# Six input projections as seven block products each, in a stage ahead of attention, and attention fed from DRAM

## The chip, the cores and the metric

The kernel runs on one core of one Trainium2 chip. The metric is the device time of one execution in microseconds (us), the median of the runs. One execution was also taken with the hardware profiler; all rows in this text come from it. The engines are named as in the profile: PE is TensorE (PEld its weight loads), DVE is VectorE, ACT is ScalarE, POOL is GpSimd, SP is SyncE, whose queue (SPq) issues most DMAs.

## The reference, cut to what matters

One decoder block on 1024 tokens of width 1024, in float32. A normed input is projected to 6664 columns, split into queries, keys and values of two kinds of attention, memory queries and gates:

```python
h = rmsnorm(x, g_mix_norm[l])
proj = jnp.einsum('bsd,de->bse', h, w_in[l])
sb_q, sb_k, sb_v, fx_q, fx_k, fx_v, f_logit, m_q, gate_logit = split_columns(proj, SPLITS)
o_sb = stick_breaking_attention(...)      # 8 heads of 64; weights from products of 1 - sigmoid, strictly causal
fq, fk = rmsnorm(fx_q, g_fox_q), rmsnorm(fx_k, g_fox_k)     # per head
o_fox = forgetting_attention(fq, fk, fx_v, log_f)            # 8 heads of 64; causal softmax with a decay
o_mem = memory_attention(rmsnorm(m_q), rmsnorm(m_k), m_v)    # 4 heads of 128; 256 memory tokens
merged = gates[0] * (o_sb @ w_branch_sb) + gates[1] * (o_fox @ w_branch_fox) + gates[2] * (o_mem @ w_branch_mem)
x = x + merged @ w_out
x = x + relu(rmsnorm(x) @ w_ff_up) ** 2 @ w_ff_down
```

Each of sb_q, sb_k, sb_v, fx_q, fx_k, fx_v and m_q has 512 columns, the gates 3072, the forget logits 8.

## The kernel before, in words

**Precision.** Every operand is split into a rounded high part (an ACT copy) and a low part (a DVE subtraction, the remainder). A product takes three passes on PE: high by high, high by low, low by high. So each product tile costs three matmuls, and each operand tile one ACT and one DVE operation. Line 951 is the remainder of a weight tile (L950 its copy).

**Order.** `Machine` (lines 182 to 278) is a planner that runs while the kernel is built. Generators yield `Op(engine, cost, fn)`, `Get(place, n)` for buffers and events; the planner keeps a clock, gives each engine the ready operation with the earliest time (plus a lateness that the caller chose), and emits instructions in that order. Operations with `side=True` (projections, gates, branches) go to PE only when no attention work is ready there. The order is fixed when the kernel is built; on the chip each engine works through its list in order and waits where a result isn't there.

**Stages, by the profile's clock.** Up to about 120 us: norms of the tokens, transposes, the first values with the first keys of stick-breaking attention, the memory keys and values. 120 to 232: memory queries and memory attention (`mem_attention`). 232 to about 590: stick-breaking attention, four pairs of heads (`sb_tile`, `unit`). 620 to about 941: forgetting attention, four pairs (`fox_tile`, `unit`). Beside the attention run the projections for later pairs (`sb_projection`, `dense_values`, `dense_fox`) and the 24 gate blocks (`dense_gate`), then the first two branch products (`dense_branch`, to about 979). Then the last branch, the output projection, and the MLP, whose up and down products, like the output projection, are already done in seven block products (P1 to P7, Winograd's form of Strassen's scheme). These later stages are outside the change.

**Projections before.** Two forms. `dense_T` (gates, stick-breaking keys and queries) has weights stationary and 512 tokens moving, and leaves the result with features on the partitions. `natural_ops` (values, memory queries, forgetting queries and keys) has 128 tokens stationary and 256 columns moving. All of these matmuls are emitted by `products`, line 1040. Results go from the PSUM bank straight into attention's tiles in SBUF: the normed ones by a copy and a square on ACT (L628, L629), a reduction (L630), a reciprocal root (seed on DVE, three steps on POOL), a scaling (L692, L1324), four transposes on PE (L700, L1277), and a copy and remainder (L702, L703, L1289 to L1303).

**Attention.** A unit is one head and 256 queries (group g of 0 to 3); large units are g = 2, 3. For each 128 queries, `sb_tile` forms scores (L772, L773), masks the diagonal (L782), takes two sigmoids (L776, L777), scans a product from the right (L791) and multiplies (L795); `fox_tile` forms scores (L815, L816), masks (L823), takes maxima (L824 and small operations to L829), exponentials (L833), a reciprocal (L838) and a scaling (L846). `unit` then transposes the weights (L874), splits them (L879 on ACT, L881 on DVE), multiplies them with the values (L894) and stores the output (L912, L913, L915). One large and one small unit are in flight; `PACE` and `units` hold each unit back until a set amount of side work was done.

**Memory.** SBUF places are pools of tiles (`HT` head tiles, `EL`/`ES` attention rows, `VV` values, `WP` three pairs of split weights, `RAW` raw weights, `OO` outputs). PSUM has eight banks: three `PP`, two `SC`, two `TR`, one `PV`.

Of the kernel before, what the change touches and what calls it, by code (L numbers as in the profile page):

```python
# [43 lines left out]
def tile_hybrid_block(  # L44
# [40 lines left out]
    C = Pool("c", st=24, st16=8, ss=4)  # L85
# [35 lines left out]
    fk_scr = dram.tile([8, 4, S], F32, name="fk_scr", tag="fk_scr")  # L121
    x2_scr = dram.tile([S, D], F32, name="x2_scr", tag="x2_scr")
# [184 lines left out]
    mem_T = [tuple(A.t(tag, [P, D], F32R).rearrange("p (k s) -> p k s", k=KD) for tag in ("e", "r")) for _ in range(2)]  # L307

    def halves(w, cols):
        res = []  # L310
        for h in range(2):
            rows = slice(h * 512, (h + 1) * 512)
            pieces, off = [], 0
            for c0, n in cols:
                pieces.append((off, w[rows, c0:c0 + n]))
                off += n
            res.append(load_w(pieces, 4, off))
        return res
# [23 lines left out]
    ES, OO = tiles(A, "es", 2, 512), tiles(A, "o", 3, 512)  # L342
    EL, RR, HT = Places([]), Places([]), Places([])
    PH, PL, OB = tiles(A, "pth", 2, 512, F32R), tiles(A, "ptl", 2, 512, F32R), tiles(A, "ob", 2, 256)
    VV = tiles(A, "v", 2, 4096, F32R)
# [163 lines left out]
    def prologue():  # L509
# [12 lines left out]
        holder["B"] = B = Pool("b", h=20)  # L522
        HT.put(*(B.t("h", [P, 512], F32R) for _ in range(20)))


    mk_made, mv_made = ([Event() for _ in range(2)] for _ in range(2))
    mq_made, mem_over = {(h, half): Event() for h in range(4) for half in range(2)}, Event()
    mq_of, mkv = {}, {}
    kv_over = Event()

    def memory():
        v = VV.free.pop()
        mkv["kh"], mkv["kl"] = (v[:, i * 1024:(i + 1) * 1024].rearrange("p (h m) -> p h m", h=4) for i in (0, 1))
        mkv["vh"], mkv["vl"] = (v[:, i * 1024:(i + 1) * 1024].rearrange("p (j e) -> p j e", j=2) for i in (2, 3))
        for ev in [spawn(mem_attention(h, half), -20.0) for c in range(2) for half in range(2) for h in (2 * c, 2 * c + 1)]:
            yield ev
# [3 lines left out]
    def mem_attention(h, half):  # L540
# [46 lines left out]
        def block(j):  # L587
# [14 lines left out]
            if j == 0:  # L602
                pv[0] = yield Get(PV)
# [1800 lines left out]
```

## Time and profile before

| | |
|---|---|
| median of 3 runs | 1741.8 us (1741.77 to 1741.9) |
| the profiled execution | 1741.96 us |
| its span, first to last instruction | 1740.2 us |
| ACT busy | 884.1 us (51%) |
| POOL busy | 117.2 us (7%) |
| granted TensorE clock | 1.0 |
| HBM read, written | 142.64 MB, 57.15 MB |
| mean DMA rate | 116 GB/s |

How to read the rows: a group row gives line, engine, operation, output and inputs by the program's names, the shape and the count; behind the first bar the busy time of the group and the mean nanoseconds of one; behind the second bar the idle time of that engine just before such instructions and what ended it. A timeline row gives the start, the duration and the instruction. A wait row says which instruction waited for which, with the sum, the number of times and the longest in us. Matmuls are pipelined, so their durations overlap; the distance between starts is what one costs.

### The profile page before, as it was taken

How to read it: one execution, taken by the hardware profiler on the slowest of the kernel's cores; microseconds unless marked ns; L12 is line 12 of the kernel's file. 1: busy time of each engine (PE TensorE's matmuls, PEld its weight loads, DVE VectorE, ACT ScalarE, POOL GpSimd, SP SyncE). 2: the span in 40 equal slices, each digit the busy share in tenths (PEclk: the TensorE clock that was granted, in tenths of full speed). 3: DMA queues.
4: the chain of work that ended last, by engine and by line, in shares of the span. 5: the costliest groups of instructions: out<-in, count | busy, mean ns of one | idle time of the engine just before them, and what ended most of it. 6: DMA issues, size and time to landing. Idle time of an engine off the chain costs nothing.

```text
span 1740.2 us, 24835 instructions
## 1 busy us (share of the span) xinstructions
PE 1726.8 (99%) x9426; PEld 1476.1 (85%) x9426; DVE 1261.5 (72%) x2014; ACT 884.1 (51%) x1553; POOL 117.2 (7%) x301
## 2 busy tenths in 40 slices
PE   9999999999999999999999999999999999999999
PEld 9889989888988899899888887878888887888887
DVE  7524578677777567666887699887777776687875
ACT  6525575555566478767974236533333344333331
POOL 0101100000000000010000000111112120000000
PEclk9999999999999999999999999999999999999999
DMA  5241121122132311212354643144444476455531
GB/s 206 73 125 52 50 87 38 42 68 57 35 89 59 90 54 32 75 49 68 113 176 134 231 157 116 49 151 155 142 151 145 152 254 230 160 201 178 193 121 73
DMA packets 135561, 201.41 MB, mean 116 GB/s; under 512 B 9681, under 2 KB 73169, under 8 KB 135441
## 3 DMA queue, kind: packets, MB, share of 16 engines
q1 hardware_dynamic: 125584, 167.05, 29.9%
q0 software_dynamic: 9856, 32.78, 5.4%
q8 instruction: 74, 1.21, 0.3%
q14 instruction: 47, 0.38, 0.1%
HBM read 142.64 MB, written 57.15 MB: 115 GB/s over the span
## 4 chain that ended last, share of the span: by engine, by line
PE 82%; issue 7%; DVE 5%; ACT 2%; POOL 2%; DMA 1%; SPq 0%; POOLq 0%; DVEq 0%; ACTq 0%
PE pp L1040 36%; PE pp L2343 7%; PE pp L1673 6%; PE pv L894 4%; PE tr L2343 4%; PE sc L2343 4%; PE tr L874 3%; PE sc L1673 3%; PE pv L2343 2%; POOL s_scr L1690 1%; PE tr L1673 1%; PE tr L1916 1%; PE sc L772 1%; PE sc L815 1%; PE sc L773 1%
## 5 line engine op out<-in xcount | busy, mean ns | idle before, releaser
L1040 PE MATMUL pp<-hi,whi 128*128 128x512 f32 x496 | 199.1, 401 | 0.0
L1040 PE MATMUL pp<-hi,wlo 128*128 128x512 f32 x496 | 195.7, 395 | 0.0
L1040 PE MATMUL pp<-lo,whi 128*128 128x512 f32 x496 | 195.1, 393 | 0.0
L1040 PE MATMUL pp<-whi,hi 128*128 128x256 f32 (+1 forms) x640 | 183.3, 286 | 0.0
L1040 PE MATMUL pp<-whi,lo 128*128 128x256 f32 (+1 forms) x640 | 179.8, 281 | 0.2 <-DVE lo L487 0.2
L1040 PE MATMUL pp<-wlo,hi 128*128 128x256 f32 (+1 forms) x640 | 179.3, 280 | 0.0
L881 DVE TENSOR_TENSOR ptl<-tr,pth 128x512 fp32r<-128x512 f32 (+1 forms) x160 | 99.3, 631 | 43.2 <-ACT pth L879 42.5
L2343 PE MATMUL pp<-h,sop 128*128 128x512 f32 x540 | 128.7, 395 | 0.4 <-DVE sop L1609 0.4
L2343 PEld LDWEIGHTS pp<-h,sop 128*128 128x128 f32 x540 | 101.2, 188 | 25.5 <-DVE sop L1609 0.9
L879 ACT ACTIVATE pth<-tr 128x512 fp32r<-128x512 f32 (+1 forms) x160 | 86.3, 555 | 70.6 <-PE tr L874 39.1
L1673 PE MATMUL pp<-h,oh 128*128 128x512 f32 x384 | 120.9, 396 | 0.7 <-ACT cu L1759 0.6
L1040 PEld LDWEIGHTS pp<-wlo,hi 128*128 128x128 f32 x640 | 120.6, 188 | 0.9
L1040 PEld LDWEIGHTS pp<-whi,hi 128*128 128x128 f32 x640 | 120.6, 188 | 0.8
L1040 PEld LDWEIGHTS pp<-whi,lo 128*128 128x128 f32 x640 | 120.5, 188 | 0.4 <-DVE lo L487 0.4
L1040 PEld LDWEIGHTS pp<-hi,wlo 128*128 128x128 f32 x496 | 93.2, 188 | 22.6
L951 DVE TENSOR_TENSOR wlo<-raw,whi 128x1024 fp32r<-128x1024 f32 (+1 forms) x72 | 87.7, 1221 | 33.9 <-ACT whi L950 33.5
L1040 PEld LDWEIGHTS pp<-lo,whi 128*128 128x128 f32 x496 | 93.3, 188 | 16.8
L1040 PEld LDWEIGHTS pp<-hi,whi 128*128 128x128 f32 x496 | 93.4, 188 | 16.3
L791 DVE TENSOR_TENSOR_SCAN r<-r,sm 128x896 f32<-128x896 f32 (+3 forms) x64 | 86.2, 1351 | 12.9 <-ACT r L776 12.4
L950 ACT ACTIVATE whi<-raw 128x1024 fp32r<-128x1024 f32 (+1 forms) x72 | 76.2, 1061 | 34.1 <-DMA raw<-w_b 24.6
L1673 PEld LDWEIGHTS pp<-h,oh 128*128 128x128 f32 x384 | 71.8, 188 | 19.1 <-ACT cu L1759 1.5
L2261 ACT ACTIVATE h<-t 128x2048 fp32r<-128x2048 f32 x16 | 30.7, 1919 | 109.9 <-DVE t L1609 97.1
(425 smaller groups left out, 4281.1 us busy)
## 6 DMA issues: line engine op xcount, KB each, us to landing
ur<-s_scr SPq DMA_DIRECT2D x26, 1024.0 KB
raw<-w_in SPq DMA_DIRECT2D x42, 512.0 KB
raw<-w_up SPq DMA_DIRECT2D x60, 256.0 KB
s_scr<-s POOLq DMA_DIRECT2D x60, 256.0 KB, 2.7
g<-w_down SPq DMA_DIRECT2D x14, 1024.0 KB
gate_scr<-o SPq DMA_DIRECT2D x48, 256.0 KB
s_scr<-cu POOLq DMA_DIRECT2D x48, 256.0 KB, 2.9
o<-gate_scr SPq DMA_DIRECT2D x32, 256.0 KB
```

Source lines behind the costliest of these rows:

```text
L772: nc.tensor.matmul(sc[:, :m], q, pair.t["k1", b, ci][:, :m], start=True, stop=False)
L791: nc.vector.tensor_tensor_scan(out=rev, data0=rev, data1=zero.to_broadcast([P, n]), initial=1.0, op0=ALU.mult, op1=ALU.add)
L874: nc.tensor.transpose(tr[:, jj * 256 + a * P:jj * 256 + (a + 1) * P], es[a][:, j * P:(j + 1) * P], ident)
L879: yield Op("ACT", act_time(512 - lo_c), lambda: nc.scalar.activation(ph[:, lo_c:], tr[:, lo_c:], AF.Copy))
L881: yield Op("DVE", dve_time(512 - lo_c), lambda: nc.vector.tensor_tensor(pl[:, lo_c:], tr[:, lo_c:], f32(ph[:, lo_c:]), ALU.subtract))
L894: nc.tensor.matmul(pv[0][:, c_:256], v_of[key][:, j, h4, :], p_[:, jj * 256 + c_:(jj + 1) * 256], start=(k == 0 and n_ == 0 and i == 0), s ...
L950: yield Op("ACT", 0.03 + act_time(m), lambda: nc.scalar.activation(hi, raw, AF.Copy))
L951: yield Op("DVE", dve_time(m), lambda: nc.vector.tensor_tensor(lo, raw, f32(hi), ALU.subtract))
L1040: nc.tensor.matmul(ps, a_, b_, start=(first and i == 0), stop=(last and i == n - 1))
L1673: nc.tensor.matmul(ps, w[a_][:, k * P:(k + 1) * P], h[b_][k], start=(first and k == 0 and i == 0), stop=(last and k == 3 and i == 2), skip ...
L2261: nc.scalar.activation(top[k][0], raw, AF.Copy)
L2343: nc.tensor.matmul(ps, a_[:, c, qs], b_[:, c, :], start=(kind in ("P1", "P2", "P7") and c == 0 and i == 0), stop=(kind in ("P2", "P4", "P3 ...
```

## The change

The six projections sbk, sbq, mq, fxk, fxq and sbv become a stage of their own ahead of attention. Each is cut into halves of tokens, contraction and columns and done in seven block products P1 to P7 instead of eight. sbk and sbq keep the weights stationary (512 columns moving); the other four keep the tokens stationary (256 columns moving).

- `sums_T` forms the sums of token blocks (operands of P5, P6, P7 and, later, P4) once for all six.
- `unit_loads` and `unit_prep` load a unit's four weight blocks, form the four block sums on DVE and split the seven operands.
- `unit_products` emits the products; `unit_evict` copies banks to SBUF (`snap`) and adds the later ones; `unit_final` splits or norms and turns the results, which are stored to DRAM. `SN` is a pool of ten tiles for all of these.
- `load_pairs`, `load_v` and `memory` bring queries, keys and values back from DRAM by DMA alone, head by head.
- `forget` works on one half at a time in three `SN` tiles. Gate 8 takes the place of the first keys beside the first values, which are now fx0; fx1 follows.
- Attention begins when the stage ends (`second_part` opens its pools). `PACE` is gone; large and small units have four row tiles each, so two of each are in flight. `fox_tile` takes the maximum of each key stretch (up to 512 keys) by itself and corrects by the exponential of the difference. Memory attention runs after the keys of the first forgetting pair are loaded.
- PSUM in attention: two `PP` and two `PV` banks. `HT` has 23 tiles, four of them made of one `WP` pair.

```diff
-    A = Pool("a", v=2, pth=2, ptl=2, e=2, es=2, r=2, o=3, ob=2)
+    E = Pool("e", side="right", sn=10)
+    MT = Pool("mt", side="right", mt=4)
+    R = Pool("r", raw=4, s1=1)
...
+    def sums_T():
+        for k in range(4):
+            (b11, b12), (b21, b22) = (...)
...
+            yield Op("DVE", dve_time(512, 512, 512), first)
+            yield Op("DVE", dve_time(512, 512), second)
+            two = [spawn(both("P6", k, t2)), spawn(both("P5", k, t1), 2.0)]
+            yield Op("DVE", dve_time(512, 512), third)
+            two.append(spawn(both("P7", k, w_), 1.0))
...
     def fox_tile(pair, b, i, e):
-        scs = yield Get(SC, len(ch))
...
+        def chunk(ci, c, cols, u):
+            sc = yield Get(SC)
...
+            yield Op("PE", mm_time(cols, cols), scores)
+            yield Op("DVE", (0.22 if c + u == n else 0.0) + dve_time(u) + SMALL, maxima)
+            yield Op("ACT", act_time(u) + 0.17, lambda: nc.scalar.activation(
+                e[:, c:c + u], sc[:, :u], AF.Exp, bias=nx[:, ci:ci + 1], accum_out=l[:, ci:ci + 1]), table=AF.Exp)
+            SC.put(sc)
...
+        if two:
+            def most():
+                nc.vector.tensor_tensor(m[:, 0:1], nx[:, 0:1], nx[:, 1:2], ALU.min)
+            yield Op("DVE", SMALL, most)
+            yield Op("ACT", 0.22, lambda: nc.scalar.activation(f, mx, AF.Exp, bias=m[:, 0:1]), table=AF.Exp)
...
+                nc.vector.tensor_tensor(t_, l, f, ALU.mult)
+                nc.vector.tensor_tensor(m[:, 1:2], t_[:, 0:1], t_[:, 1:2], ALU.add)
+                nc.vector.reciprocal(t_[:, 0:1], m[:, 1:2])
+                nc.vector.tensor_scalar(f, f, t_[:, 0:1], None, ALU.mult)
...
     def units(large):
-        yield kv_over
-        for ev in mq_made.values():
-            yield ev
-        base = machine.side
+        yield ready
...
-                while machine.side - base < PACE[c] + (PACE[c + 1] - PACE[c]) * n / 8:
-                    yield Sleep(0.5)
-                spawn(unit(pair, b, g, es))
+                spawn(unit(pair, b, g, es), 0.0 if large else -6.0)
+
+    def load_pairs():
+        yield ready
+        for c, pair in enumerate(pairs):
...
+            for b in range(2):
+                got = yield Get(HT, 8 if fox else 6)
...
+                machine.fire(pair.made[b])
...
+    PROJ = ("sbk", "sbq", "mq", "fxk", "fxq", "sbv")
...
+    def unit_prep():
+        yield kv_taken
+        for u in PROJ:
+            for kind in KINDS:
...
+                    for out_, a_, b_, op in ((s1, a21, a22, ALU.add), (a21, a11, a21, ALU.subtract),
+                                             (a11, s1, a11, ALU.subtract), (a12, a12, a11, ALU.subtract)):
+                        yield Op("DVE", dve_time(1024), lambda: nc.vector.tensor_tensor(out_, a_, b_, op))
+                pair = yield Get(WP)
...
+                yield from split(pair[0][:, :1024], pair[1][:, :1024], src)
...
+    def unit_products(u, turned_w):
...
+            for kind in KINDS:
+                yield prepped[u, kind]
+                pair, w = p_ops[u, kind]
+                for q in range(2):
...
+                    if kind in ("P6", "P5", "P3"):
+                        yield snapped[u, {"P6": "P1", "P5": "P6", "P3": "P5"}[kind], q]
+                    if kind == "P4":
+                        yield added[u, "P5", q]
...
+    def hand_back():
+        for place in (PP, PP, SC, SC, PV, PV):
+            place.put((yield Get(BK)))
...
+    def second_part():
...
+        yield last_sums
+        yield prepped[PROJ[-1], "P4"]
+        holder["T"].close()
+        R.close()
+        opened("A", (HT, "h", 12, 512, F32R), (VV, "v", 2, 2048, F32R), (EL, "e", 4, D, F32), (RR, "r", 3, D, F32))
+        machine.fire(ready)
+        yield last_turn
+        for ev in proj_over:
+            yield ev
+        yield forgot
+        holder["T4"].close()
+        E.close()
+        opened("A2", (PH, "pth", 2, 512, F32R), (PL, "ptl", 2, 512, F32R), (OB, "ob", 2, 256, F32),
+               (ES, "es", 4, 512, F32), (OO, "o", 3, 512, F32), (HT, "h", 7, 512, F32R))
...
+    gates = [dense_gate(n, may_gate) for n in (*range(16, 24), *range(0, 8), *range(9, 16))]
+    h_tasks = [dense_values("fx0", C_FXV, None, first_gate), dense_values("fx1", C_FXV + 256, fn)]
...
+    h_tasks += kv_tasks
+    h_tasks += [unit_products(u, u in ("sbk", "sbq")) for u in PROJ]
     h_tasks += gates
...
-    PACE = [62 * min(c, 4) + 58 * max(c - 4, 0) + 14 * (c == 8) for c in range(9)]
```

More of the change, by code (lines that the diff above doesn't have):

```diff
@@ L971, in loader @@
     def loader(tasks):
-        two = False
         while tasks:
-            t = next((t for t in tasks if not (two and len(t.loads) == 2) and t.may()), None)
-            two = False
+            t = next((t for t in tasks if t.may()), None)
             if t is None:
@@ L1193, in sb_projection @@
[L1193 to L1204 removed]
+                evict(last, put(ps, t // 2), ps, SC)
```

861 lines of the change are left out of this document (476 added, 385 removed).

## The prediction

> **What bounds the kernel now.** I read the page first, then who made TensorE (PE) wait, then the pace of PE's instructions, then stretches of the span.
>
> ```profile
> span 1740.2 us, 24835 instructions
> ...
> PE 1726.8 (99%) x9426; PEld 1476.1 (85%) x9426; DVE 1261.5 (72%) x2014; ACT 884.1 (51%) x1553; POOL 117.2 (7%) x301
> ...
> PE 82%; issue 7%; DVE 5%; ACT 2%; POOL 2%; DMA 1%; SPq 0%; POOLq 0%; DVEq 0%; ACTq 0%
> ...
> L1040 PE MATMUL pp<-hi,whi 128*128 128x512 f32 x496 | 199.1, 401 | 0.0
> ...
> L1040 PE MATMUL pp<-whi,hi 128*128 128x256 f32 (+1 forms) x640 | 183.3, 286 | 0.0
> ```
>
> PE is busy for 99% of the span and carries 82% of the chain of waits. The two L1040 rows are one third each of the input projections (three passes per product): 3 x 496 matmuls of 512 columns and 3 x 640 of 256.
>
> A busy PE need not be a full one, so I looked at its waits (twelve rows, the first and the last shown) and at the starts of consecutive matmuls.
>
> ```profile
> PE tr L874 <- DVE ptl L881: 1.5, 1, 1.5
> ...
> PE sc L815 <- ACT e L833: 0.2, 1, 0.2
> ```
>
> ```profile
> 100.19 0.40 PE L1040 MATMUL pp<-hi,whi 128*128 128x512 f32 x1
> ...
> 103.70 0.39 PE L1040 MATMUL pp<-hi,whi 128*128 128x512 f32 x1
> ```
>
> ```profile
> 622.05 0.28 PE L1040 MATMUL pp<-whi,hi 128*128 128x256 f32 x1
> ...
> 626.55 0.28 PE L1040 MATMUL pp<-whi,lo 128*128 128x256 f32 x1
> ```
>
> ```profile
> 247.37 0.62 PE L874 MATMUL tr<-ident,e 128*128 128x128 f32 x4
> 247.75 0.36 PE L894 MATMUL pv<-pth,v 128*128 128x256 f32 x1
> ```
>
> Fifteen matmuls of 512 columns start within 3.51 us, so one costs 0.234 us, not the 0.40 it is shown to last. Between 622.05 and 626.55 there are 38 steps of 256 columns: 0.118 us each. Four transposes take 0.38 us, 0.095 each. The longest PE wait is 1.5 us. So what is taken from PE comes off the time, unless the work that remains stops arriving in time.
>
> ```profile
> 87.00:120.00 33.00, 32.55 (x190) 28.25 (x189) 10.09 (x10) 8.93 (x12) 0.45 (x3) 1.00 0.45 128
> 232.00:590.00 358.00, 357.93 (x2123) 313.67 (x2122) 273.60 (x404) 211.84 (x422) 4.11 (x13) 1.00 0.22 62
> ...
> 620.00:853.00 233.00, 232.72 (x1628) 215.28 (x1627) 163.98 (x409) 177.76 (x366) 16.44 (x72) 1.00 0.20 59
> 853.00:941.00 88.00, 85.31 (x476) 72.81 (x475) 74.11 (x176) 67.33 (x139) 0.00 (x0) 1.00 0.45 142
> ```
>
> The columns after the length are busy PE, PE's weight loads, VectorE (DVE), ScalarE (ACT), GpSimd, then granted clock, DMA share, GB/s. In the stick-breaking attention (232 to 590) DVE is 76% busy, in the forgetting attention (620 to 853) 70%, in its end (853 to 941) 84%. PE is full because projections and gates fill the gaps of attention there. That is the reserve which the change rearranges.
>
> **What the change does to PE.** A projection of 512 columns takes 192 matmuls of 512 columns (8 contraction tiles x 4 x 2 x 3 passes) or 384 of 256. With 7 block products it takes 7 x 2 x 4 x 3 = 168, or 336. Two units (sbk, sbq) run in the wide form: 2 x 24 x 0.234 = 11.2 us less. Four (mq, fxk, fxq, sbv) run in the narrow form: 4 x 48 x 0.118 = 22.7 us less. Together **33.9 us** less. The normed units turn 3 x 32 blocks, as many as the old code does for the same columns, and the columns of scores and values stay. So nothing is added on PE.
>
> **What the change adds beside PE**, priced with these rows.
>
> ```profile
> L881 DVE TENSOR_TENSOR ptl<-tr,pth 128x512 fp32r<-128x512 f32 (+1 forms) x160 | 99.3, 631 | 43.2 <-ACT pth L879 42.5
> L951 DVE TENSOR_TENSOR wlo<-raw,whi 128x1024 fp32r<-128x1024 f32 (+1 forms) x72 | 87.7, 1221 | 33.9 <-ACT whi L950 33.5
> L791 DVE TENSOR_TENSOR_SCAN r<-r,sm 128x896 f32<-128x896 f32 (+3 forms) x64 | 86.2, 1351 | 12.9 <-ACT r L776 12.4
> ...
> L824 DVE TENSOR_REDUCE st<-sc 128x1 f32<-128x512 f32 (+2 forms) x96 | 53.3, 556 | 14.5 <-PE sc L816 12.2
> ...
> L795 DVE TENSOR_TENSOR e<-e,r 128x895 f32<-128x895 f32 (+3 forms) x32 | 32.5, 1015 | 0.7
> ...
> L913 DVE TENSOR_TENSOR ob<-ob,pv 64x256 f32<-64x256 f32 x64 | 25.9, 404 | 15.3 <-ACT ob L912 14.7
> ...
> L823 DVE TENSOR_TENSOR sc<-sc,above 128x128 f32<-128x128 f32 x64 | 18.6, 290 | 9.6 <-PE sc L816 9.5
> L782 DVE TENSOR_TENSOR sc<-sc,above 128x128 f32<-128x128 f32 x64 | 18.4, 290 | 10.3 <-PE sc L773 10.2
> ...
> L795 DVE TENSOR_TENSOR es<-es,r 128x127 f32<-128x127 f32 (+3 forms) x32 | 15.4, 484 | 1.2
> ...
> L560 DVE TENSOR_REDUCE st<-sc 128x2 f32<-128x512 f32 x16 | 11.0, 685 | 6.4 <-PE sc L149 6.4
> ...
> L630 DVE TENSOR_REDUCE ss<-o 128x8 f32<-128x512 f32 x16 | 10.9, 680 | 10.8 <-ACT o L629 10.5
> L838 DVE RECIPROCAL st<-st 128x1 f32<-128x1 f32 x64 | 10.3, 161 | 4.8 <-ACT es L833 3.2
> ...
> L1324 DVE TENSOR_TENSOR r<-r,st 128x1024 f32<-128x1024 f32 x8 | 9.8, 1224 | 8.0 <-POOL st L368 8.0
> ...
> L703 DVE SCALAR_TENSOR_TENSOR h<-tr,sm,h 128x512 fp32r<-128x512 f32 x8 | 6.0, 750 | 5.8 <-ACT h L702 5.8
> ```
>
> ```profile
> 1014.56 0.68 DVE L1609 TENSOR_TENSOR g<-g 128x512 f32<-128x512 f32 x1
> ...
> 1016.96 0.68 DVE L1609 TENSOR_TENSOR cu<-g,cu 128x512 fp32r<-128x512 f32 x1
> ```
>
> In a dense stretch four such steps take 2.40 us: 0.60 us of DVE for an operation shown as 0.68. Sums of durations are thus up to 12% too high when the engine is full. I give both.
>
> *The token sums.* The sums of the halves and their splits are 40 operations of 512 columns before the units (40 x 0.68 = 27 us of DVE) and 16 later. They fall among the values and the memory keys; from 87 to 120 DVE is busy 10.1 of 33 us. Cost nothing; without that cover the third product (P6) would start late by what remains, at most 27 us.
>
> *Start of the units.* The first weight block needs an ACT copy and an L951 remainder (1.22 us) with a 5.6 us memory-value product left to cover it. Between 0 and some 3 us; I take **1.5**.
>
> *The three normed units (mq, fxk, fxq).* Per unit: 4 block sums and 7 remainders of 1024 columns, 11 x 1.22 = 13.4 us; six additions of a bank, 6 x 0.68 = 4.1; eight finals of a reduction (0.68), half an L1324 (0.61), an L703 (0.75) and two small operations (2 x 0.16), 8 x 2.36 = 18.9. That is 36.4 us of DVE beside 336 x 0.118 = 39.6 us of PE: 92%, or 81% at the dense pace. The forget gate falls into fxk with ten operations at 0.68 and two scans (1.35 as L791's mean): 9.5 us more, while it holds three of the ten SN tiles. Over three units 118.7 us of DVE stand against 118.8 of PE. Low end 0 (dense pace, 105 us), high end: DVE 85% busy at full durations, 118.7 / 0.85 = 140, 21 us late. I take **3**, nearer the dense pace, because snapshots are ordered ahead and the next unit's first three blocks are prepared ahead. For sbk, sbq and sbv the finals are an L881 each: 13.4 + 4.1 + 8 x 0.68 = 23 of 39 us, no cost.
>
> *Attention and gates.* PE work: 23 gates x 48 x 0.234 = 258 us. Per head 9,728 columns of scores and 9,216 of values, 18,944 x 0.234 / 512 = 8.66 us; 16 heads 138.5; 576 transposes 54.7; memory attention 96 narrow and 48 wide matmuls and 64 transposes, 28.6. Attention is 222 us, with gates 480; the two branches behind add 384 x 0.234 = 90, in all 570 us. DVE work: the attention rows sum to 349.6 us (L881, L791, L824, both L795, L913, L823, L782); L838 and four like groups of 32, 10.3 + 20.6; memory about 31 (L560's 11.0, 16 remainders of 0.68, 32 scalings of 256 columns priced at L913's 0.40 less a quarter). The maxima by stretch add three small operations to 32 wide tiles, 15 us; the gates' remainders 23 x 1.22 = 28. That is 455 us at full durations, 400 at the dense pace, against 480 of PE. Attention's PE work goes ahead of gates in the order, and gates may not end first: branch 0 waits for the memory output, for the last pair's loads and for free head tiles. With 400 to 455 us, attention is over or in its last pair when the gates are used up (480), so idle is small. No row shows DVE at such a load in attention for long. Low end: -2.7 us, PE's idle from 853 to 941 (88.00 less 85.31), which may go. High end: the rival below. I take **5**.
>
> *DMA.* Results go to DRAM, about 16 stores per unit on SP's queue, and come back in 12 issues per stick-breaking head and 16 per forgetting head, with eight for the values: 232 loads, 33 MB in 480 us, 70 GB/s beside the 62 of the row above. The 853 to 941 row moved 142 at a 0.45 share, so bytes cost nothing. But SP waits in order, behind stores:
>
> ```profile
> SPq L915 <- DVE ob L913: 247.9, 45, 26.5
> ```
>
> A head's loads can sit behind such a store for up to 26.5 us. With 23 head tiles, of which a head takes 6 or 8, two heads lie ahead, each 25 us of DVE or more (400 / 16). This is covered, except while the memory attention holds tiles; it is in the 5 above.
>
> **Sum.** The profiled execution took 1741.96 us (span 1740.2 and 1.76 outside), 0.16 above the median of 1741.8, so I change nothing for that. 1741.96 - 33.9 + 1.5 + 3 + 5 = 1717.6, say **1718**.
>
> **The rivals.** *DVE limits the normed units* (their high end): 21 us for 3, 1718 + 18 = 1736. For it: 100% DVE at full durations and ten SN tiles. Against: the dense pace.
>
> *Attention starves PE (the slower side).* Nothing spreads attention any more, and once the gates are gone PE waits for DVE and ACT. The stage has 570 us of PE and, with the branches' 59 us (8 x 1.22, 48 operations and 24 splits at 0.68), 459 to 514 us of DVE. The saving is gone when the stage lasts 604 us, that is with DVE at 76% (dense) or 85% (full durations). At the 70% of the row of 620 to 853, and 459 us, it lasts 656: 86 us late, 1708 + 86 = 1794. For it: 70% and 76% were seen. Against: those stretches were paced by the planner beside projections with one large and one small unit in flight, and the unpaced one shows 84%.
>
> *Nothing gained:* about 30 us of these losses together, 1738 to 1746, near no change.
>
> *PE's clock drops in pauses.* If PE paused at six places (start, three units, handover, branches) and came back at half pace for fifteen matmuls (3.5 us) each, that is 21 us more: 1739. Every window row here shows a granted clock of 1.00, and no wait above 1.5 us in which it could have dropped. The Trainium skill (TensorE: Matmul & The Clock Gate, Part 1) states such a gate, half rate after an idle window of about 3.4 us; no run here shows it.
>
> **How the numbers follow.** Forecast (1703 to 1727) 0.54; normed units (1727 to 1738) 0.15; clock 0.03; no gain 0.06; starved attention (1746 to 1794) 0.22. A change within 0.2% (3.5 us) is about what a measurement of this kernel can tell from none. Faster is 0.54 + 0.15 + 0.03 = 0.72, same 0.06, slower 0.22. The range reaches from the forecast's low end, 1703 (no stall and the 2.7 us gained, less 2), to 1750, so that 0.2 stay outside.
>
> **What would show it.** Right: 144 fewer wide-equivalent matmuls (6 x 24), PE still 98% or more, units of 39 us, no PE wait above some 3 us. The normed rival: PE waits on DVE in the stage of the units, units of 45 us. The slow rival: PE waits for L881- or L846-like results after the last gate, DVE below 76% there. Wrong altogether: PE idle at the change of stages, where tiles are given back (waits on DMA), or a granted clock below 1.00.

## The result and the profile after

The changed kernel takes **1765.4 us** (median of four runs, 1765.15 to 1765.67) against 1741.85 us for the kernel before on the same chip: a ratio of 1.0134, 95% interval 1.0116 to 1.0152. It is 1.3% slower, where 1718 us were forecast. PE does have the fewer matmuls that were forecast (9186 against 9426); the time is elsewhere. The lines of the page after that answer to those shown of before:

```profile
span 1763.9 us, 25496 instructions
...
PE 1708.9 (97%) x9186; PEld 1450.5 (82%) x9186; DVE 1338.7 (76%) x2243; ACT 895.2 (51%) x1612; POOL 172.9 (10%) x445
...
PEclk9999999998999999999999999999999999999999
...
PE 53%; issue 15%; POOL 8%; DVE 6%; DMA 3%; ACT 3%; SPq 1%; POOLq 0%; ACTq 0%; DVEq 0%
```

Two numbers account for all of it. PE is idle for 1763.9 - 1708.9 = 55.0 us of the span; before it was 1740.2 - 1726.8 = 13.4, so 41.6 us were added. And PE is busy for 1708.9 us, where the work that is left should take 1726.8 - 33.9 = 1692.9: 16.0 us too much, at a mean granted clock that fell from 1.00 to 0.992. The sum, 1742.0 - 33.9 + 41.6 + 16.0 = 1765.7, is the profiled execution's 1763.9 and the 1.8 around it.

The slice of the clock row that shows 8 is the tenth, 397 to 441 us. To see where the idle time lies, I asked for stretches of the span (columns: length, busy PE, its weight loads, DVE, ACT, POOL, granted clock, DMA share, GB/s).

```profile
0.00:125.00 125.00, 115.08 (x881) 109.28 (x882) 100.19 (x182) 63.77 (x111) 7.84 (x32) 0.99 0.54 178
...
200.00:385.00 185.00, 167.05 (x1373) 162.55 (x1372) 125.78 (x209) 85.33 (x127) 89.51 (x289) 0.99 0.41 124
385.00:440.00 55.00, 42.84 (x213) 35.76 (x212) 34.13 (x49) 26.86 (x57) 0.00 (x0) 0.88 0.71 214
440.00:700.00 260.00, 259.77 (x1519) 224.94 (x1517) 223.55 (x429) 200.32 (x432) 0.00 (x0) 1.00 0.44 125
700.00:900.00 200.00, 193.81 (x1134) 166.59 (x1133) 157.05 (x496) 173.75 (x429) 0.00 (x0) 0.99 0.48 146
```

Two stretches stand out: the normed units with the values' unit behind them (200 to 385: 18.0 us idle) and the change from units to attention (385 to 440: 12.2 us idle, clock 0.88). Attention itself, from which the main slower rival came, is full: 0.2 us idle of 260. Who made PE wait, in the whole span (total, times, longest):

```profile
PE tr L723 <- DVE sn L716: 12.9, 18, 1.9
PE pp L812 <- ACT e L817: 12.2, 2, 7.5
PE tr L723 <- DVE sn L730: 3.7, 2, 2.1
PE pp L1412 <- DVE wlo L1047: 3.6, 2, 3.1
PE sc L1133 <- ACT pth L675: 3.4, 1, 3.4
```

**The normed units.** PE stands 18 times at the four transposes of a normed block (L723), for DVE's scaling by the root (L716). DVE is busy only 125.8 of 185 us there, so it isn't full. What is it waiting for? DVE's own waits in 200 to 385, and the groups of POOL there:

```profile
DVE sn L716 <- POOL st L361: 28.9, 22, 2.0
```

```profile
L358 POOL TENSOR_TENSOR st<-st 128x8 f32<-128x8 f32 (+1 forms) x72 | 25.2, 350 | 147.7 <-DVE st L352 142.3 <-DVE st L351 1.7
L359 POOL TENSOR_TENSOR st<-st,st 128x8 f32<-128x8 f32 (+1 forms) x72 | 22.6, 314 | 5.7
L360 POOL TENSOR_SCALAR st<-st 128x8 f32<-128x8 f32 (+1 forms) x72 | 21.3, 295 | 6.3
L361 POOL TENSOR_TENSOR st<-st,st 128x8 f32<-128x8 f32 (+1 forms) x72 | 20.3, 283 | 6.0
```

The root is twelve small steps on GpSimd (L358 to L361, three times), which the planner prices at 12 x 0.2 = 2.4 us. They last 0.28 to 0.35 us in the mean. Their timeline tells why, beside DVE's:

```profile
230.58 0.20 POOL L359 TENSOR_TENSOR st<-st,st 128x4 f32<-128x4 f32 x1
230.87 0.19 POOL L360 TENSOR_SCALAR st<-st 128x4 f32<-128x4 f32 x1
...
232.21 1.04 POOL L360 TENSOR_SCALAR st<-st 128x4 f32<-128x4 f32 x1
```

```profile
231.98 1.22 DVE L1047 TENSOR_TENSOR wlo<-raw,whi 128x1024 fp32r<-128x1024 f32 x1
```

Undisturbed, a step lasts 0.20 us and the next begins 0.28 us later: 12 x 0.28 = 3.4 us for a root. A step that begins during one of DVE's 1024-column operations with two inputs in SBUF ends only when that operation does (232.21 + 1.04 = 233.25, against 231.98 + 1.22 = 233.20). Of the 288 steps 42 last more than 0.3 us, and each of these ends within 0.1 us of the end of a VectorE operation. The Trainium skill (SBUF — State Buffer, "SBUF: two separate sides") states the rule: VectorE and GpSimd share a pair of ports which one instruction holds to its end, and a VectorE operation with two SBUF inputs takes it. These rows agree, with 1.04 us where the step alone takes 0.20. So a root takes some 3.4 us and, by the summed busy time (89.4 us for 24 roots, 31.8 more than 288 x 0.20), 1.3 us more on average; the order written out by hand has the scaling and the transposes in place after 2.4.

**The change of stages.** ACT's waits from 370 to 450 us, and SyncE's queue there:

```profile
ACT whi L1046 <- DMA raw<-w_in: 11.3, 2, 6.9
...
ACT ob L956 <- DMA o_scr<-ob: 4.2, 1, 4.2
```

```profile
389.52 0.59 SPq L1032 DMA_DIRECT2D v<-v_sb  x1
390.20 1.08 SPq L1207 DMA_DIRECT2D v_sb<-sn  x2
391.33 0.94 SPq L1054 DMA_DIRECT2D raw<-w_in  x1
392.33 9.32 SPq L996 DMA_DIRECT2D h<-sbk_scr  x8
```

ACT takes its list in order. At 394 it comes to the copy of a gate's weights (L1046), which have not landed, and stands for 6.9 us; the sigmoids of the stick-breaking tiles, which give the score banks back, are behind it, so PE stands at L812, for 4.7 us. A second stop of ACT, 4.3 us for weights (the rest of the 11.3) and then 4.2 us for the store that frees an attention output's buffer (`ob`), ends with PE's longest pause, 7.5 us. What PE does after that pause:

```profile
432.89 0.80 PE L812 MATMUL pp<-h,h 128*128 128x512 f32 x1 [7.46 <-ACT e L817]
...
435.12 0.63 PE L1133 MATMUL pp<-lo,whi 128*128 128x512 f32 x1
435.54 0.63 PE L1133 MATMUL pp<-hi,wlo 128*128 128x512 f32 x1
```

Matmuls of 512 columns start 0.42 to 0.43 us apart instead of 0.234, some 5 us long. The granted clock is 0.50 there, and in five other stretches before PE's last matmul:

```profile
123.69:127.10 3.41, 3.41 (x10) 2.62 (x9) 3.41 (x6) 1.58 (x2) 0.00 (x0) 0.50 0.70 183
311.42:314.83 3.41, 3.41 (x19) 3.41 (x18) 3.04 (x6) 2.16 (x4) 2.24 (x7) 0.50 0.48 126
403.58:406.99 3.41, 3.21 (x10) 2.73 (x11) 3.06 (x6) 1.35 (x5) 0.00 (x0) 0.50 0.64 218
427.47:437.71 10.24, 4.82 (x13) 3.54 (x14) 5.83 (x8) 4.19 (x9) 0.00 (x0) 0.50 0.56 157
721.02:724.43 3.41, 3.37 (x10) 2.39 (x11) 1.02 (x3) 3.40 (x8) 0.00 (x0) 0.50 0.63 210
1099.90:1103.31 3.41, 3.06 (x12) 2.67 (x13) 3.01 (x6) 3.38 (x7) 0.00 (x0) 0.50 0.76 285
```

PE works for 21.3 us in these six, at half pace, which loses 10.6 of the 16.0 us; the other 5.4 are not assigned. The pauses ahead of them are 3.1, 2.1, 4.7, 7.5, 3.4 and 2.4 us. The Trainium skill (TensorE: Matmul & The Clock Gate, Part 1), which the prediction cited for its clock rival, states half rate after an idle window of about 3.4 us and until a busy one of about that length. The trace agrees on the 3.4 us at half rate (310 to 315 us reads 0.66 as a whole, so half clock lasts no longer there); but pauses of 2.1 and 2.4 us, shorter than that idle window, were enough here.

### The profile page after: what moved, and what is told of

Read it like the earlier page. It is cut to its first block, busy times and chain, and to the rows that moved or that the text cites. A ratio compares the mean times of both kernels' runs of the same rounds, so it can differ in the third digit from the quotient of the medians.

```text
span 1763.9 us, 25496 instructions
## 1 busy us (share of the span) xinstructions
PE 1708.9 (97%) x9186; PEld 1450.5 (82%) x9186; DVE 1338.7 (76%) x2243; ACT 895.2 (51%) x1612; POOL 172.9 (10%) x445
## 4 chain that ended last, share of the span: by engine, by line
PE 53%; issue 15%; POOL 8%; DVE 6%; DMA 3%; ACT 3%; SPq 1%; POOLq 0%; ACTq 0%; DVEq 0%
PE pp L1133 17%; PE pp L2510 7%; PE tr L2510 3%; PE sc L2510 3%; POOL s_scr L1857 3%; PE tr L921 3%; PE pv L2510 2%; PE pv L938 2%; PE sc L938 2%; POOL st L358 1%; PE pp L1840 1%; POOL st L359 1%; POOL st L360 1%; POOL st L361 1%; DVE h L1776 1%
## 5 line engine op out<-in xcount | busy, mean ns | idle before, releaser
L1133 PE MATMUL pp<-hi,whi 128*128 128x512 f32 x368 | 148.8, 404 | 0.0
L1133 PE MATMUL pp<-lo,whi 128*128 128x512 f32 x368 | 145.9, 396 | 0.0
L1133 PE MATMUL pp<-hi,wlo 128*128 128x512 f32 x368 | 145.5, 395 | 0.0
L1047 DVE TENSOR_TENSOR wlo<-raw,whi 128x1024 fp32r<-128x1024 f32 (+1 forms) x82 | 100.1, 1221 | 45.6 <-ACT whi L1046 45.5
L1046 ACT ACTIVATE whi<-raw 128x1024 fp32r<-128x1024 f32 (+1 forms) x82 | 86.4, 1056 | 87.8 <-DMA raw<-w_b 35.1
L928 DVE TENSOR_TENSOR ptl<-tr,pth 128x512 fp32r<-128x512 f32 (+1 forms) x160 | 98.6, 627 | 21.3 <-ACT pth L926 20.1
L831 DVE TENSOR_TENSOR_SCAN r<-r,sm 128x896 f32<-128x896 f32 (+5 forms) x64 | 85.6, 1346 | 7.9 <-ACT r L816 7.9
L1133 PEld LDWEIGHTS pp<-hi,wlo 128*128 128x128 f32 x368 | 69.6, 189 | 16.7
L1840 PE MATMUL pp<-h,ol 128*128 128x512 f32 x192 | 76.0, 396 | 0.0
L1833 ACT ACTIVATE oh<-raw 128x512 fp32r<-128x512 f32 x64 | 39.4, 625 | 61.8 <-DVE raw L1776 61.8
L2510 PE MATMUL sc<-h,sop 128*128 128x512 f32 x264 | 63.4, 395 | 0.0
L2510 PE MATMUL tr<-h,sop 128*128 128x512 f32 x264 | 63.4, 395 | 0.0
L1133 PE MATMUL pp<-h,whi 128*128 128x512 f32 x192 | 63.0, 396 | 0.0
```

Of the source, the lines that this page charges most:

```text
L831: nc.vector.tensor_tensor_scan(out=rev, data0=rev, data1=zero.to_broadcast([P, n]), initial=1.0, op0=ALU.mult, op1=ALU.add)
L928: yield Op("DVE", dve_time(512 - lo_c), lambda: nc.vector.tensor_tensor(pl[:, lo_c:], tr[:, lo_c:], f32(ph[:, lo_c:]), ALU.subtract))
L1046: yield Op("ACT", 0.03 + act_time(m), lambda: nc.scalar.activation(hi, raw, AF.Copy))
L1047: yield Op("DVE", dve_time(m), lambda: nc.vector.tensor_tensor(lo, raw, f32(hi), ALU.subtract))
L1133: nc.tensor.matmul(ps, a_, b_, start=(first and i == 0), stop=(last and i == n - 1))
L1833: nc.scalar.activation(h_, src, AF.Copy)
```

## Experiments

Theory U: the length of the root's chain makes PE wait in the normed units. Rival V: DVE has too much to do there. Theory S: at the change of stages, one queue that works in order holds the gate weights. Rival B: the bytes do. All times are medians, beside 1765.4 us of the changed kernel and 1741.4 to 1741.8 us of the kernel before in the same sets of runs. The changed kernel itself was timed in one set only; the kernel before differs by 0.5 us at most from set to set.

**1. Only the root's price in the plan.**

```diff
-        yield Op("POOL", 12 * 0.2, steps)
+        yield Op("POOL", 12 * 0.375, steps)
```

> Only the planner's price of the root's twelve GpSimd steps is raised, from 2.4 to 4.5 us, near what the trace of the changed kernel shows (12 x 0.27 to 0.38 us); every instruction stays, the order written out by hand changes. Theory U (the four transposes of a normed block stand in PE's list too early, because the root is slower than planned): PE's idle time from 200 to 385 us falls from 17 us to under 8, and the time from 1765 to 1747-1757 us. Rival V (VectorE itself is too full in the normed units): the order changes nothing, 1763-1768 us.

Measured: 1757.4 us (four runs, 1752.6 to 1762.4), ratio to before 1.0092 (1.0070 to 1.0113), at the edge of theory U. PE's waits at L723 for L716 went from 12.3 to 1.3 us in 200 to 400, and its idle time in 200 to 385 from 18.0 to 10.2. A wait of 4.8 us for a weight remainder (`pp L1412 <- DVE wlo L1047`) took the place of part of it. The order can avoid the stand, but not the length of the chain.

**2. The twelve steps on VectorE.**

```diff
-                nc.gpsimd.tensor_tensor(a_, a, a, ALU.mult)
+                nc.vector.tensor_tensor(a_, a, a, ALU.mult)
...
-        yield Op("POOL", 12 * 0.2, steps)
+        yield Op("DVE", 12 * SMALL, steps)
```

> The twelve steps of each root run on VectorE instead of GpSimd, and are planned there; 24 roots put 24 x 12 x 0.16 us = 46 us more on VectorE in the three normed units, which takes it from about 65% to about 100% busy there at full durations. Theory U: the root then takes the time it is planned to take, PE's waits at the transposes go, 1748-1758 us. Rival V: VectorE becomes later by up to 46 us, 1775-1810 us.

Measured: 1798.9 us, 1.0333 (1.0316 to 1.0350). Theory V's number. The stretch of the normed units:

```profile
200.00:385.00 185.00, 149.89 (x1179) 147.27 (x1179) 150.94 (x456) 71.97 (x102) 0.51 (x1) 0.90 0.30 87
```

VectorE is at 150.9 of 185 us, 82%, and PE at 149.9, at a clock of 0.90. So U alone is too simple: VectorE has room in the changed kernel (68%), but not for these 49.6 us more (1388.3 us in the whole span for 1338.7). Its share alone does not make it late, though: run 3 shows 82% with PE never waiting.

**3. No refinement of the root.**

```diff
-        yield Op("POOL", 12 * 0.2, steps)
-        return y1
+        return y0.bitcast(F32)
```

> The three refinement steps of the root are left out (the scale is the seed alone, so the outputs are not the reference's). Nothing else of the normed blocks changes. Theory U: PE's waits at the transposes vanish, idle from 200 to 385 us below 5 us, 1745-1753 us. Rival V: VectorE has as much to do as before, so 1762-1767 us.

Measured: 1735.2 us, 0.9965 (0.9954 to 0.9975), 30.3 us less than the changed kernel and more than U asked for.

```profile
200.00:385.00 185.00, 180.56 (x1461) 176.91 (x1459) 137.90 (x227) 97.14 (x153) 0.52 (x1) 0.98 0.51 157
```

PE is idle for 4.4 us here, not 18.0. From the first matmul of mq to the last of fxq, the three normed units alone, first in the changed kernel, then in this run:

```profile
191.40:338.94 147.54, 133.86 (x1098) 130.10 (x1096) 105.03 (x169) 71.66 (x101) 76.44 (x249) 0.99 0.42 125
191.69:320.83 129.14, 129.14 (x1102) 128.93 (x1100) 105.46 (x172) 72.00 (x102) 0.52 (x1) 1.00 0.46 139
```

VectorE's work is the same, 105 us. Without the twelve GpSimd steps PE has no idle time in these units (13.7 us before) and the full clock, beside a VectorE that is 82% busy. That settles U against V for the changed kernel. The three units take 18.4 us less. Of the rest, 3.8 us are PE's two waits for the sigmoids at the change of stages (8.4 us for 12.2), so the 30 us overlap with the loss of the next run.

**4. The pair loads from another queue.**

```diff
-                        nc.sync.dma_start(f32(t[k][rows_, :]), src)
+                        nc.gpsimd.dma_start(f32(t[k][rows_, :]), src)
```

with the same in `load_v`, and these issues planned on POOL.

> The loads of the heads' queries, keys and values (load_pairs, load_v) are issued from GpSimd's queue instead of SyncE's; bytes and planned order stay. Theory S (at the change of stages ScalarE stands before the gate weights because their load and the stores are issued behind some 0.6 us per pair load in one queue): the two waits of ScalarE on raw<-w_in there (11.3 us) go below 4 us, the granted clock stays at 1.00, 1748-1757 us. Rival B (the bytes of the first heads fill the DMA engines whatever queue issues them): the waits stay, 1762-1768 us.

Measured: 1746.7 us, 1.0032 (1.0020 to 1.0045): 18.7 us less, slightly more than S asked for. The change of stages with the same bytes:

```profile
385.00:440.00 55.00, 53.93 (x305) 46.35 (x304) 46.86 (x71) 36.47 (x79) 26.39 (x50) 1.00 0.83 231
```

The DMA engines are busier than before (0.83 for 0.71), and PE is idle for 1.1 us instead of 12.2, at a clock of 1.00. Rival B falls as the cause of PE's loss. ACT's wait for weights is 3.3 us in place of 11.3; the fetch that SyncE issued at 391.33 goes out at 385.75, the next at 399.69 in place of 416.51. A fetch still takes long beside the pair loads: ACT begins with the first of these weights 12.0 us after their issue here, 9.9 us in the changed kernel. That leaves ACT its 3.3 us.

**5. The root on ScalarE and VectorE.**

```diff
-        r = yield from rsqrt_ops(ss, n)
+        z = stat(n)
+        yield Op("ACT", 0.22, lambda: root(z, ss), table=AF.Sqrt)
+        r = yield from rsqrt_quick(ss, z, n)
```

> The root of the normed blocks is made by one square root on ScalarE and five small steps on VectorE (the way in which the kernel's token norms make theirs) instead of two steps on VectorE and twelve on GpSimd: 24 + 4 x 3 x 0.16 us = some 14 us more for VectorE, about 1.3 us from the sum of squares to the scaling instead of 3.5 to 4.5. Theory U (the length of the root's chain, not VectorE's load, makes PE wait): most of the 30 us that leaving the refinement out saved, 1738-1748 us. Theory V (any more work on VectorE is late, as the 46 us more of the run with the steps on VectorE were): 1762-1780 us.

Measured: 1748.1 us (seven runs, 1746.2 to 1756.2), 1.0042 (1.0027 to 1.0058), 17.3 us less, at the edge of theory U. A short chain helps even with more work on VectorE (1347.3 us for 1338.7, 8.6 more where 14 were expected).

**6. Both repairs.** The edits of 4 and 5.

> The root on ScalarE and VectorE, and the pair loads from GpSimd's queue, together. If the two losses are separate, their gains add: 18.7 us (the queue) and 17 to 27 us (the root) off 1765.4, 1720-1730 us, granted clock 1.00, PE idle in all below 30 us. If they share time (a stage that ends earlier only meets the next wait), 1735-1746 us.

Measured: **1735.6 us**, 0.9965 (0.9952 to 0.9978), faster than both kernels. It lies at the low end of the second expectation: 29.8 us less, where 36.0 would be the sum, so the two losses shared some 6 us. Its idle time is 1733.8 - 1701.7 = 32.1 us.

**7. Only the plan's price of SyncE's DMAs,** 0.55 us each.

```diff
-        yield Op("SP", issue, fn, 0.0)
+        yield Op("SP", 5.5 * issue, fn, 0.0)
```

and so for the stores (1.1 us for two at once, 0.55 for one; the keys' four loads of a half at 2.2).

> Only the planner's price of a DMA on SyncE's queue is raised, from 0.1 us (or less) to 0.55 us each, as the trace shows it; every transfer stays on SyncE and every instruction stays. Theory S1 (the time that issuing takes, unknown to the planner, is what puts ScalarE's list out of order): most of the 18.7 us that the second queue gave comes back, 1747-1755 us. Theory S2 (a queue that works in order holds the gate weights behind pair loads that wait for tiles and bytes, whatever the plan): 1760-1770 us.

Measured: 1759.3 us, 1.0100 (1.0085 to 1.0115): 6.2 us less, between the two, and nearer S2. PE still stands 6.8 us once at L812. A right price gives a third of what a second queue gives.

**8. The old maxima.** As 6, with `fox_tile` of the kernel before (cut to its core).

```diff
-            sc = yield Get(SC)
+        scs = yield Get(SC, len(ch))
...
-                nc.vector.tensor_scalar(nx[:, ci:ci + 1], mx[:, ci:ci + 1], -1.0, None, ALU.mult)
+                nc.vector.tensor_tensor(nx, mx[:, 0:1], mx[:, 1:2], ALU.max)
+                nc.vector.tensor_scalar(nx, nx, -1.0, None, ALU.mult)
```

> As the run with both repairs, but with the forgetting attention's maxima as in the kernel before: one maximum over all key stretches, both score banks taken at once. It tells what the maxima by key stretch alone are worth. If they help PE (score banks come free sooner), this is 3-15 us slower than the run with both; if their three small VectorE steps and the second ScalarE scaling only cost (ScalarE is 95% busy there), 3-10 us faster; within 3 us: worth nothing.

Measured: 1746.7 us, 1.0031 (1.0018 to 1.0044), 11.0 us slower than 6. The forgetting attention in this run, then in run 6:

```profile
700.00:900.00 200.00, 190.98 (x1102) 163.16 (x1101) 152.40 (x426) 153.78 (x365) 40.98 (x78) 0.98 0.48 140
```

```profile
700.00:900.00 200.00, 198.28 (x1151) 170.55 (x1151) 156.59 (x478) 165.25 (x405) 35.20 (x66) 1.00 0.51 147
```

The maxima by key stretch are worth their three small operations: PE's idle time falls from 9.0 to 1.7 us here. In the code each score bank is then taken and released by itself instead of two at once, which fits, though no run separates that from the rest of the edit.

**9. One large unit in flight.** As 6.

```diff
-(EL, "e", 4, D, F32)
+(EL, "e", 2, D, F32)
```

> As the run with both repairs, but with two tiles instead of four for large units, so that one large unit of attention is in flight and not two. If two are what keeps TensorE full from 440 to 900 us (idle 3.9 of 460 us there), one gives longer waits for scores and values: 1745-1790 us. If ScalarE and VectorE set attention's pace anyway and gates fill the gaps, no change: 1733-1738 us.

Measured: 1784.5 us, 1.0246 (1.0228 to 1.0264), 48.9 us slower than 6. The same stretch:

```profile
700.00:900.00 200.00, 177.78 (x961) 148.64 (x960) 143.73 (x452) 151.01 (x376) 50.41 (x95) 0.90 0.45 135
```

This is the starved attention that the prediction feared, and two large units in flight are what prevents it. About half of the loss is idle time of PE (56.2 us for 32.1), the other half busy time (25.2 us more) at a mean clock of 0.982.

**10. The first weight block earlier.** As 6.

```diff
-            w2 = yield from weights(2, made)
             if c and not keys:
                 machine.fire(kv_taken)
+            w2 = yield from weights(2, made)
```

> As the run with both repairs, but the first weight block of the units is prepared before the last memory values' weights are taken, not after. PE's 3.1 us wait for wlo at about 118 us should go if the late start of that block is its cause: 1732-1734 us. If VectorE, which the token sums fill there (14.5 of 15 us from 115 to 130), is the cause, the wait only moves: 1735-1738 us.

Measured: 1735.9 us, 0.9969 (0.9957 to 0.9982), no change. The wait for `wlo` stays (3.0 us), so a late start of that block is not its cause. It is not that block's remainder either that PE waits for, as the part on the start of the units shows.

**11. Only the weights from another queue.** As 5, for the weights of gates and branches.

```diff
-            yield from transfer(lambda: fetch(raw, load), P * kk * n * 4)
+            yield from transfer(lambda: fetch(raw, load, nc.gpsimd), P * kk * n * 4, queue="POOL")
```

> As the run with the root on ScalarE alone (1748 us), but only the weights of gates and branches are loaded from GpSimd's queue; the pair loads and all stores stay on SyncE. If the wait at the change of stages is the gate weights held in SyncE's queue, this gives what the pair loads' move gave: 1734-1738 us. If it is the pair loads themselves or the stores that come late in that queue, nothing changes: 1746-1751 us. If the bytes are the cause, nothing changes either.

Measured: 1756.9 us, 1.0091 (1.0075 to 1.0107), 8.8 us slower than 5. None of the outcomes that I had written down. ACT's longest wait from 370 to 450, and the queue that caused it:

```profile
ACT ob L958 <- DMA o_scr<-ob: 13.8, 1, 13.8
```

```profile
400.05 4.93 SPq L998 DMA_DIRECT2D h<-sbk_scr  x8
405.02 3.66 SPq L998 DMA_DIRECT2D h<-sbq_scr  x4
...
420.59 0.54 SPq L961 DMA_DIRECT2D o_scr<-ob  x1
```

ACT's wait for weights is gone, and it stands at the next thing in the same queue: the attention output's buffer (`ob`), whose store is issued at 420.59, behind more than twenty pair loads. So S has to be widened: it is not the weights but all that shares the pair loads' queue.

**12. Gate weights one task further ahead.** As 6.

```diff
-            while queue:
+            while len(queue) > (t in gates):
```

> As the run with both repairs, but the planner takes gate weights one task further ahead. What is left of the change of stages (PE 3.5 us, ScalarE's wait for gate weights) goes: 1731-1734 us; if the weight tiles, of which two pairs are left after the units, don't allow it, or ScalarE then stands at the next load: 1735-1739 us.

Measured: 1759.1 us, 1.0095 (1.0077 to 1.0113), 23.5 us slower than 6. Five waits for a weight copy (`whi`), 13.2 us in all and 7.0 the longest, are new in PE's list, four of them in the units (L1414). That fits the second expectation, that gates and units share too few weight tiles.

**13. Shorter token sums.** As 6.

```diff
-                nc.vector.tensor_tensor(w_, f32(b12[1]), f32(b11[1]), ALU.subtract)
-                nc.vector.tensor_tensor(t1, t1, w_, ALU.add)
...
-                nc.vector.tensor_tensor(t2, t2, f32(b22[1]), ALU.add)
...
-                nc.vector.tensor_tensor(w_, w_, f32(b11[1]), ALU.subtract)
```

> As the run with both repairs, with the token sums cut from seven VectorE operations per contraction tile to three (the remainders of the halves are left out of them, so the sums lack their low parts): 16 x 0.6 = 10 us less for VectorE before the units. If the sums are what makes the opening idle, PE's idle to 125 us falls from 9.6 us towards 5 and the time to 1730-1733 us. If they are covered, as the forecast had it, 1734-1738 us.

Measured: 1735.1 us, 0.9958 (0.9943 to 0.9973), no change to be told from run 6, though VectorE had 7 us less to do in the first 125 us. PE's idle time there fell from 9.6 to 7.8 us, but its wait of 3.1 us stayed. The edit shortens the sums for P5, P6 and P7 and leaves those for P4 as they are, so it does not speak for all of them.

**14. The price of the pair loads.** As 6; the same for the queries.

```diff
-spawn(transfer(k0_, 4 * HD * 2048, 0.3, queue="POOL"), -20.0)
+spawn(transfer(k0_, 4 * HD * 2048, 2.1, queue="POOL"), -20.0)
```

> As the run with both repairs; only the planner's price of a pair load's issue on GpSimd's queue is raised, from 0.3 us for two to four loads to 0.53 each, as the trace shows it. If the wrong price is what leaves the wait of 3.5 us at the change of stages and 1.7 us in the forgetting attention, 1731-1734 us; if the order is already right, 1734-1738 us.

Measured: 1734.3 us (1732.2 to 1736.7), 0.9957 (0.9943 to 0.9971): the lowest median, but its runs overlap those of run 6 (1734.2 to 1736.7). No difference shown.

**15. An eighth product.** As 6.

```diff
+                        if kind == "P4":
+                            todo, cost = todo + todo, 2 * cost
```

> As the run with both repairs, but each of the six projections runs its seventh block product twice (it is then added twice, so the outputs are not the reference's): 24 wide or 48 narrow matmuls more per projection, 33.9 us of TensorE. If TensorE's work counts one for one, 1767-1771 us. If the units wait for VectorE's and ScalarE's work anyway, the added matmuls fill waits and the rise is smaller: 1752-1765 us, with the saving of the seven products in doubt by as much.

Measured: 1751.9 us, 1.0056 (1.0041 to 1.0071). With 33.9 us of matmuls added, the time rises by 16.2. Run 6 in the stretch of the normed units, then this one, and this one's page:

```profile
200.00:375.00 175.00, 168.03 (x1372) 165.94 (x1371) 134.25 (x282) 94.44 (x157) 10.97 (x21) 0.97 0.46 141
```

```profile
200.00:375.00 175.00, 175.00 (x1488) 174.56 (x1487) 132.16 (x271) 93.83 (x148) 6.90 (x13) 1.00 0.44 133
```

```profile
PE 1728.8 (99%) x9426; PEld 1476.5 (84%) x9426; DVE 1349.0 (77%) x2321; ACT 906.7 (52%) x1644; POOL 200.2 (11%) x365
```

With eight products PE has no idle time in that stretch and the full clock; with seven it waits for 7.0 us and runs at 0.97. Over the whole span PE is idle for 20.8 us instead of 32.1, and its busy time rises by 27.1 us instead of 33.9, at a clock of 0.999 instead of 0.995. So about half of the time of the matmuls taken away had only filled waits for other engines and kept the clock up.

## Why the prediction was wrong, step by step

**PE's work: the count right, its worth not.** 240 fewer matmuls stand in the page. But the step "what is taken from PE comes off the time, unless the work that remains stops arriving in time" met its exception: in the repaired kernel 16.2 of the 33.9 us come off (run 15).

**Start of the units and token sums: the cost came in the other term.** The step had 1.5 us for a wait on the first weight block, and nothing for the token sums. The units begin at 108.23 us, and from 100 to 120 PE never waits more than 0.4 us. Its wait of 3.1 us comes at the third product, P6 (copy of its weights on ACT, then VectorE, then PE):

```profile
118.36 1.04 ACT L1046 ACTIVATE whi<-raw 128x1024 fp32r<-128x1024 f32 x1
```

```profile
120.04 0.69 DVE L566 TENSOR_TENSOR sn<-hi,h 128x512 f32<-128x512 f32 x1
...
121.36 0.69 DVE L568 TENSOR_TENSOR sn<-sn,sn 128x512 f32<-128x512 f32 x1
121.97 1.22 DVE L1047 TENSOR_TENSOR wlo<-raw,whi 128x1024 fp32r<-128x1024 f32 x1
```

```profile
123.25 0.50 PE L1412 MATMUL pp<-h,wlo 128*128 128x512 f32 x1 [3.07 <-DVE wlo L1047]
```

The copy is ready at 119.40, but the remainder (L1047) stands in VectorE's list behind three operations of the sums for P4 (L566 to L568, 2.0 us). These are among the "16 later" operations of the prediction; the order put them at the start of the first unit, long before P4. P6 starting late is what the prediction named for sums without cover, though for want of the sums and not of the weights. No run moves these sums (runs 10 and 13 left them in place, and the wait with them), so this is read from the timeline and not tested. The opening to 125 us is 9.9 us idle against 4.2 in the kernel before:

```profile
0.00:125.00 125.00, 120.84 (x819) 110.58 (x820) 67.54 (x115) 60.06 (x96) 7.72 (x32) 1.00 0.43 135
```

The cause of the other 2.7 us of this difference stays open.

**Three normed units: the step that failed most.** It took 3 us, with 21 as the high end. Leaving the refinement out gave 30.3 us back (run 3), 18.4 of them within these units. The step priced VectorE's load and asked whether 118.7 us of work fit beside 118.8 of PE. The load was even less, 105.0 us, and would have fitted: in run 3 PE, with its transposes busy for 129.1 us there, does not wait. But the step did not list the root's twelve GpSimd steps at all, and never added up the chain from the sum of squares to the transposes, on which an order written out by hand depends. A row that it printed held the sign: in the kernel before, VectorE stood 8.0 us for GpSimd ahead of eight scalings (L1324, `8.0 <-POOL st L368 8.0`). The rival "DVE limits the normed units" named the right place, and its signs came, PE waiting on DVE and units of about 45 us and more (44.8, 49.3 and 53.5), but for another reason: VectorE was 68% busy and itself stood 28.9 us for GpSimd. More work on it does cost time (run 2), but the changed kernel was not at that limit.

**Attention and gates: right.** The forecast had 5 us; PE idles 0.2 us from 440 to 700, and 6.2 from 700 to 900, of which 3.4 is one wait in the memory attention. The starved attention (1746 to 1794) did not come; with one large unit in flight it would have (run 9). So the result lies in that rival's range for other reasons. One part was luck: the maxima by stretch stood in the sum as 15 us of VectorE work alone, and the kernel with both repairs is 11.0 us faster with them (run 8).

**DMA: nearly right on bytes, wrong on the queue.** "Bytes cost nothing" holds for PE (run 4: 1.1 us idle from 385 to 440 at a DMA share of 0.83). "Covered [...] it is in the 5 above" does not: the cover, two heads ahead, was worked out for the middle of the stage, while at its start no head lies ahead, and the first heads' loads, the gate weights and the stores come at once in one queue. Moving the pair loads out of it gave 18.7 us. The prediction had this among its signs of "wrong altogether", PE idle at the change of stages, without a price.

**The clock: the right mechanism at too low a chance.** It was priced at 21 us, six pauses of 3.5 us each, with a chance of 0.03, because no wait above 1.5 us had been seen before. Six stretches at half clock came, from the first unit to past 1100 us, but each of 3.4 us costs only half its length: 10.6 us in all, of 16.0 us of added busy time. A forecast of new waits has to price the clock with them.

**The sum.** Run 6 takes 1735.6 us: 1742.0 - 33.9, plus 32.1 - 13.4 = 18.7 us of idle time, plus 1701.7 - 1692.9 = 8.8 us of added busy time, at a mean clock of 0.995. That is still 17.6 above the forecast, and of the 33.9 us run 15 misses 17.7. The range, to 1750, holds the kernel with both repairs (1735.6) and those with one (1746.7 and 1748.1), but not the changed one: two losses of this size together, and the clock on top, were no case in it.

## What to carry to other kernels

Where an order is written out by hand, add up the chain of each new result over all its engines, at the durations of the trace and not of the plan: an engine far from full still makes the next one wait. At a change of stages, list what stands in each DMA queue at that moment; a burst of loads belongs in another queue than the stores and weights that hand buffers back. And test what fewer matmuls are worth by adding them back: here half of their time had only filled waits.

## What was not expected of the hardware

- A GpSimd step on 128x4 or 128x8 values takes 0.20 us alone, and 1.04 to 1.25 us if it begins early in one of VectorE's 1024-column operations with two SBUF inputs (1.22 us). The longest, 1.7 us, was held through two VectorE operations in a row.
- Undisturbed GpSimd steps of 0.20 us start 0.28 us apart.
- SyncE needs some 0.6 us per issue for the pair loads (12 in 7.5 us from 408.34 on); GpSimd issues them at 0.53 us each. The eight of SyncE that took 9.3 us from 392.33 on include time in which its queue stood for other DMAs.
- Half clock came in stretches of 3.4 us, and of 10.2 us at the longest pause. Pauses from 2.1 us on could bring it, but not each did: after the wait of 3.1 us at the third product there was one in run 15 and none in run 6 (granted clock 1.00 from 115 to 130 us).
